# Weights queued behind x, activations behind state evictions, and an fp32 GLU with the normaliser's products among its blocks

## The chip, the cores and the metric

The kernel runs on one core of a Trainium2 chip. A core has a matrix engine (TensorE, PE in the rows, with its weight loads as PEld), three vector-like engines (VectorE = DVE, ScalarE = ACT, GpSimd = POOL), and SyncE (SP), which here only issues DMAs. Each engine works its own queue in order; semaphores tie the queues together, and 16 DMA engines carry the transfers. The metric is the device time of one execution, in microseconds (us): 1270.35 before the change, the median of 3 runs (1269.5 to 1273.52).

## The reference

One encoder layer on 256 positions with 16 learned meta tokens ahead (L = 272), model width 2048, all in float32:

```
hn = rmsnorm(h, norm_mix_g)
u_s5, qk_in, v_in, o_pre, gates_pre = split(hn @ w_in)      # 1024, 1024, 1024, 1024, 32 columns
# S5 half: 64 groups of 16 inputs, 64 complex states, a forward and a backward scan
y = s5_scan(u, fwd) + s5_scan(u, bwd) + d_skip * u
y = gelu(y)
y_s5 = rmsnorm(y * sigmoid(y @ w_glu + b_glu), s5_out_g)    # w_glu: 1024 x 1024
# mLSTM half: 8 heads, q and k of 64, v of 128, both directions
qk = silu(dwconv3(qk_in))
h_ml = (num_fwd / max(|den|, exp(-m))) + the same backward, then per-head rms norm, * head_g
y_ml = sigmoid(o_pre) * h_ml
h = h + concat(y_s5, y_ml) @ w_out                          # 2048 x 2048
hn = rmsnorm(h, norm_ffn_g)
h = h + (silu(dwconv3(hn @ w_gate)) * (hn @ w_up)) @ w_down # width 5632
return rmsnorm(h, final_g)[16:]
```

## The kernel before

Activations are kept transposed: 128 features on the partitions, positions along the free axis. A weight matrix comes in pieces of 128 x 1024 floats (512 KB), eight 128 x 128 blocks each. Products with weights are done in one of two ways. `whole` (L311 to L326) loads a piece and uses it as plain fp32; the trace shows each such product as two records. `stream` and `piece` (L232 to L250) load a piece as `raw`, ScalarE copies it into `hi` in the rounded type f32r (L247), VectorE forms `lo = raw - hi` (L248), and `mm3` does three f32r products, hi\*hi, hi\*lo, lo\*hi (L263 to L265). Both take their buffers from the same nine slots (three tags of three).

The order of work is not written out by hand. The framework's scheduler gives each engine a queue: it follows the order of the program as a priority, `hp()` raises the priority of what stands in it, and `behind(a, b)` puts a after b in an order without making it wait for b's result. A queue is then worked strictly in order.

The stages that the change touches, in order of time:

- *The start.* x comes as X in four quarters (`x_load`, L301), the first in two parts; `pd` is the last of these loads. ScalarE squares each (L308), VectorE scales it by g_mix (L310), the tables of the S5 recurrence are worked out from `par`, R (the norm's factor) is formed, and X is multiplied by it (L1002). `whole` loads the pieces of w_in for the first blocks; only its third piece is put behind `pd`.
- *Blocks of w_in* (`win_block`, L475: 16 fp32 products of 128 x 128 by 128 x 272, 32 records). Eight `u_block`s feed the S5 half: their result goes through `un` (L520 to L527) to DRAM (`ud`) and back as U, one pair of blocks at a time. `qk_block` (L658 on) gives a block of q or k: ScalarE evicts it twice (L665, L666), VectorE does the convolution `qt` (L668, L669), ScalarE takes SiLU into `q_sb` (L671) or `kE`, `kO`.
- *Input products of the S5* (`s5_in`, that is `in_coefs` and `in_proj`). `in_coefs` loads `tcf` (L534, a ring of two buffers, two loads each) and VectorE forms the coefficients `ic` (L542, `pp` L543). `in_proj` does 64 small products with U (L562) and ScalarE evicts them into the state ST (L568). They run in pairs m = 0,1 to 6,7.
- *The recurrence* on VectorE: `rec_local` (steps L575 to L578), `rec_carry` (L598 to L601), `rec_spread`.
- *Gate rows.* `gate_rows` (L615 on) forms the mLSTM's gate rows and sends them through DRAM: `nmd` (L638), `nmm` (L640, two), `cmd` (L649, two) and back as cM (L650, two; VectorE adds a constant to it, L651). `ml_meta` (L709 on) reads `nb` and `nb2` from `nmm` (L722, L723) and takes two exps, `pm` (L726, L727). Although this stands late in the program, the scheduler does it as soon as its data is there, around 55 to 77 us.
- *The heads* (`ml_head`), and then the GLU of the S5 half. `s5_gelu` takes the GELU of U in place and keeps it also as an f32r pair `yg`. `s5_glu` does eight blocks of eight `mm3` steps, a sigmoid, a product with U (L962), a split into y5 (L286) and a running sum of squares.
- *The normaliser* `ml_norm`, a generator (L787 on). Its first step sends the reciprocals to DRAM (`rd`). Each of the next eight loads `rb`, multiplies a head's `num` by it on VectorE (L800), adds the two directions on GpSimd, squares on ScalarE (L803) and sums with a product on TensorE (L804). All eight are called behind `s5_glu`.
- *w_out, first half*: 16 blocks of eight `mm3` steps with y5. The other half and the FFN follow.

## Time and profile before

| | before |
|---|---|
| median of 3 runs | 1270.35 us |
| the profiled execution: its time | 1271.38 us |
| its span, first to last instruction | 1269.6 us |
| mean granted TensorE clock | 0.984 |
| busy: PE, PEld | 1212.6 us (96%), 1082.7 us (85%) |
| busy: DVE, ACT, POOL | 796.1 us (63%), 535.3 us (42%), 221.6 us (17%) |
| chain that ended last | PE 79%, DVE 13%, DMA 4%, issue 2%, ACT 2% |

Busy is the time in which an engine has at least one instruction in work, waiting not counted; matmuls are pipelined, so records overlap. An idle time in front of an instruction is put down to what released it ("<-ACT ST L568" is the eviction in line 568 on ScalarE). The granted clock is the share of full speed that TensorE was allowed in a stretch; full is 2.4 GHz and the lower level 1.2. Engine averages hide the stages, since the limit changes along the program: so the rows further down are read by stretch.

### The profile page before, as it was taken

To read this page: it belongs to the slowest core of one execution; us is meant where nothing else is said; L and a number is where in the kernel's file an instruction comes from. 1 tells how busy PE (TensorE), PEld (TensorE's weight loads), DVE (VectorE), ACT (ScalarE), POOL (GpSimd) and SP (SyncE) were. 2 spreads that over 40 slices of the span, in tenths; PEclk is the share of its full clock that TensorE was granted. 3 is DMA by queue.
4 is the path that set the end of the run, shared out by engine and by line. 5 is a ranking of instruction groups with operands and counts; after the bars stand their busy time and mean duration, and the time that the engine had idled before them with its cause. 6 is when DMAs were issued, how large, how long until landed. Compare 5 with 4: busy or idle time off the path is not lost.

```text
span 1269.6 us, 21964 instructions
## 1 busy us (share of the span) xinstructions
PE 1212.6 (96%) x8865; PEld 1082.7 (85%) x8865; DVE 796.1 (63%) x1094; ACT 535.3 (42%) x865; POOL 221.6 (17%) x325
## 2 busy tenths in 40 slices
PE   5889997999998999999999999999999999999995
PEld 3768786787787799999999998889999999998884
DVE  4845999441238778766666665555666666665554
ACT  2622221125444546544444444334444444445542
POOL 3400000011315433122111220000221122111111
PEclk9989999999998999999999999999999999999998
DMA  8496544464345565555555556666555555556663
GB/s 316 128 302 195 186 148 140 125 183 133 92 133 176 161 191 183 182 185 181 188 186 184 184 184 184 193 185 198 185 187 185 183 183 183 185 177 195 188 190 112
DMA packets 84410, 227.79 MB, mean 179 GB/s; under 512 B 16508, under 2 KB 31380, under 8 KB 84308
## 3 DMA queue, kind: packets, MB, share of 16 engines
q1 hardware_dynamic: 76404, 220.67, 54.8%
q0 software_dynamic: 896, 3.28, 0.8%
q10 hardware_dynamic: 7008, 2.43, 0.8%
q8 instruction: 70, 1.15, 0.4%
q14 instruction: 32, 0.26, 0.1%
HBM read 219.81 MB, written 5.48 MB: 177 GB/s over the span
## 4 chain that ended last, share of the span: by engine, by line
PE 79%; DVE 13%; DMA 4%; issue 2%; ACT 2%; SPq 0%; DVEq 0%; POOL 0%; ACTq 0%
PE ps_mm L274 26%; PE ps_mm L275 13%; PE ps_mm L264 8%; PE ps_mm L475 8%; PE ps_mm L263 8%; PE ps_mm L265 8%; DMA tcf<-td 1%; PE ps_s L264 1%; PE ps_s L263 1%; PE ps_s L265 1%; DVE ST L578 1%; DVE t L576 1%; PE ps_s L886 1%; DVE t L575 1%; DVE ST L577 1%
## 5 line engine op out<-in xcount | busy, mean ns | idle before, releaser
L248 DVE TENSOR_TENSOR lo<-raw,hi 128x1024 fp32r<-128x1024 f32 (+1 forms) x312 | 393.5, 1261 | 233.0 <-ACT hi L247 226.9
L247 ACT ACTIVATE hi<-raw 128x1024 fp32r<-128x1024 f32 (+1 forms) x312 | 324.0, 1038 | 398.3 <-PE ps_mm L274 174.7
L475 PE MATMUL ps_mm<-X,wf 128*128 128x272 f32 (+1 forms) x1056 | 260.3, 405 | 18.7 <-DVE X L310 9.8
L475 PEld LDWEIGHTS ps_mm<-X,wf 128*128 128x128 f32 x1056 | 204.9, 197 | 62.0 <-DVE X L310 19.1
L274 PE MATMUL ps_mm<-X,hi 128*128 128x512 f32 x704 | 251.7, 399 | 0.0
L274 PE MATMUL ps_mm<-a,hi 128*128 128x512 f32 x704 | 244.1, 390 | 0.0
L264 PE MATMUL ps_mm<-X,hi 128*128 128x258 f32 x704 | 200.5, 285 | 0.0
L263 PE MATMUL ps_mm<-X,hi 128*128 128x258 f32 x704 | 199.1, 283 | 0.0
L275 PE MATMUL ps_mm<-a,lo 128*128 128x256 f32 x704 | 198.6, 282 | 0.0
L275 PE MATMUL ps_mm<-X,lo 128*128 128x256 f32 x704 | 198.1, 281 | 0.0
L265 PE MATMUL ps_mm<-X,lo 128*128 128x258 f32 x704 | 197.8, 281 | 0.0
L274 PEld LDWEIGHTS ps_mm<-X,hi 128*128 128x128 f32 x704 | 132.2, 188 | 30.1
L274 PEld LDWEIGHTS ps_mm<-a,hi 128*128 128x128 f32 x704 | 132.2, 188 | 27.6
L1144 POOL TENSOR_TENSOR gt<-gt,R 128x256 f32<-128x256 f32 x44 | 59.6, 1355 | 488.8 <-ACT gt L1143 488.8
L265 PEld LDWEIGHTS ps_mm<-X,lo 128*128 128x128 f32 x704 | 134.8, 191 | 0.0
L275 PEld LDWEIGHTS ps_mm<-X,lo 128*128 128x128 f32 x704 | 134.2, 191 | 0.0
L263 PEld LDWEIGHTS ps_mm<-X,hi 128*128 128x128 f32 x704 | 132.5, 188 | 1.9
L275 PEld LDWEIGHTS ps_mm<-a,lo 128*128 128x128 f32 x704 | 133.4, 190 | 0.0
L264 PEld LDWEIGHTS ps_mm<-X,hi 128*128 128x128 f32 x704 | 132.9, 189 | 0.0
L1149 DVE TENSOR_TENSOR u<-ps_mm,gt 128x512 f32<-128x512 f32 x44 | 30.4, 692 | 29.2 <-PE ps_mm L275 27.4
L1150 POOL TENSOR_TENSOR gt<-u 128x256 f32<-128x256 f32 x44 | 34.8, 790 | 40.5 <-DVE u L1149 40.5
L1138 DVE TENSOR_TENSOR gx<-ps_mm,R 128x258 f32<-128x258 f32 x44 | 18.8, 427 | 27.3 <-PE ps_mm L265 27.3
(333 smaller groups left out, 1401.9 us busy)
## 6 DMA issues: line engine op xcount, KB each, us to landing
raw<-wg SPq DMA_DIRECT2D x88, 512.0 KB, 3.9
raw<-wu SPq DMA_DIRECT2D x88, 512.0 KB, 4.2
wf<-win SPq DMA_DIRECT2D x65, 512.0 KB, 4.0
raw<-wd SPq DMA_DIRECT2D x64, 512.0 KB, 3.6
raw<-wout SPq DMA_DIRECT2D x32, 512.0 KB, 4.1
raw<-wd SPq DMA_DIRECT2D x32, 384.0 KB, 3.8
tcf<-td SPq DMA_DIRECT2D x16, 256.0 KB, 6.9
bc<-bcs SPq DMA_DIRECT2D x8, 512.0 KB, 3.7
```

Source lines behind the costliest of these rows:

```text
L247: S.activation(hi[:, a:b], raw[:, a:b], AF.Copy)
L248: V.tensor_tensor(out=lo[:, a:b], in0=raw[:, a:b], in1=hi.bitcast(F32)[:, a:b], op=ALU.subtract)
L263: nc.tensor.matmul(out_ap, h, xh, start=(first and i == 0), stop=False)
L264: nc.tensor.matmul(out_ap, h, xl, start=False, stop=False)
L265: nc.tensor.matmul(out_ap, l, xh, start=False, stop=(last and i == n - 1))
L274: nc.tensor.matmul(both[:, :, :cols], h, x, start=(i == 0), stop=False)
L275: nc.tensor.matmul(both[:, 1, :cols], l, x[:, 0, :], start=False, stop=(i == n - 1))
L475: last_o[0] = nc.tensor.matmul(p[:, :L - t0], w[k // 8][:, k % 8 * P:k % 8 * P + P], X[:, k, t0:], start=(k == 0), stop=(k == KD - 1))
L1138: V.tensor_tensor(out=x[:, :N], in0=p[:, :N], in1=R2, op=ALU.mult)
L1144: G.tensor_tensor(out=t, in0=t, in1=R2[:, 2:], op=ALU.mult)
L1149: V.tensor_tensor(out=u, in0=p.rearrange("p (j t) -> p j t", j=2), in1=t.unsqueeze(1).to_broadcast([P, 2, SEQ]), op=ALU.mult)
L1150: G.tensor_tensor(out=t, in0=u[:, 0, :], in1=u[:, 1, :], op=ALU.add)
```

## The change

1. `whole` puts its third to tenth piece behind the last load of x, where before it was the third alone.
2. `in_coefs` keeps its last `tcf` load in `last_tc`, and `gate_rows` puts `nmd`, `nmm` and `cmd` behind it. The loads of cM, `nb` and `nb2` read what those write, so they go with them.
3. `in_proj` keeps its last eviction of ST in `last_st`. `qk_block` no longer takes its SiLU itself but returns a function `act` that does, behind `last_st`; it is called behind the input products of the pair. The exp of `pm` is put behind `last_st` too.
4. `s5_gelu` no longer makes the f32r pair. `s5_glu` takes w_glu through `whole` and does one fp32 product of 128 x 128 by 128 x 272 a step, straight from U, instead of three in f32r.
5. From its fourth block on, `s5_glu` calls the normaliser once a block (five times); three calls stay behind it.

Lines from there on are numbered 2 to 5 higher in the changed kernel.

```diff
@@ -230,2 +230,4 @@
     last_o = [None]
+    last_st = [None]
+    last_tc = [None]
 
@@ -323,3 +325,3 @@
             last_raw[0] = nc.sync.dma_start(w[:, a:b], src[:, a:b])
-            if plain[0] == 3:
+            if 3 <= plain[0] <= 10:
                 behind(last_raw[0], pd)
@@ -533,5 +535,5 @@
         for g in range(2):
-            nc.sync.dma_start(t[64 * g:64 * g + 64].rearrange("p q r k -> p (q r k)"),
-                              tb["td"][:, g, 4 * m:4 * m + 4].rearrange("s j d r p -> s (j d r p)")
-                              .unsqueeze(0).to_broadcast([16, 4, 1024]))
+            last_tc[0] = nc.sync.dma_start(t[64 * g:64 * g + 64].rearrange("p q r k -> p (q r k)"),
+                                           tb["td"][:, g, 4 * m:4 * m + 4].rearrange("s j d r p -> s (j d r p)")
+                                           .unsqueeze(0).to_broadcast([16, 4, 1024]))
         if m >= 4:
@@ -567,3 +569,3 @@
                 j = 4 * m + q0 + o
-                S.copy(ST[:, 2 * j:2 * j + 2, :, 1:], pv[o])
+                last_st[0] = S.copy(ST[:, 2 * j:2 * j + 2, :, 1:], pv[o])
 
@@ -637,5 +639,5 @@
         nmm = dr.tile([2, 8, 16, L], F32, name="nmm")
-        nc.sync.dma_start(nmd, M[:40])
+        behind(nc.sync.dma_start(nmd, M[:40]), last_tc[0])
         for d in range(2):
-            nc.sync.dma_start(nmm[d], M[32 * d:32 * d + 8].unsqueeze(1).to_broadcast([8, 16, L]))
+            behind(nc.sync.dma_start(nmm[d], M[32 * d:32 * d + 8].unsqueeze(1).to_broadcast([8, 16, L])), last_tc[0])
         cT = lq.tile([P, 2, 40], F32, name="cT")
@@ -648,3 +650,3 @@
         for d in range(2):
-            nc.sync.dma_start(cmd[d], c[32 * d:32 * d + 8, 0:16])
+            behind(nc.sync.dma_start(cmd[d], c[32 * d:32 * d + 8, 0:16]), last_tc[0])
             nc.sync.dma_start(cM[:, d:d + 1], cmd[d].rearrange("h (s o) -> (h s) o", o=1))
@@ -669,7 +671,10 @@
             V.scalar_tensor_tensor(out=tt, in0=x[:, t0 + 2:L + 2], scalar=vc("qw", 16 + m), in1=tt, op0=ALU.mult, op1=ALU.add)
-        if m < 4:
-            S.activation(q_sb[:, m, :], t[:, T0:], AF.Silu)
-        else:
-            S.activation(kE[0:64, m - 4, :], t[0:64], AF.Silu)
-            S.activation(kO[64:128, m - 4, :], t[64:128], AF.Silu)
+
+        def act():
+            if m < 4:
+                behind(S.activation(q_sb[:, m, :], t[:, T0:], AF.Silu), last_st[0])
+            else:
+                behind(S.activation(kE[0:64, m - 4, :], t[0:64], AF.Silu), last_st[0])
+                S.activation(kO[64:128, m - 4, :], t[64:128], AF.Silu)
+        return act
 
@@ -725,3 +730,3 @@
         cM = rows["cM"]
-        S.activation(pm[:, 1:N], nb[:, 1:N], AF.Exp, bias=cM[:, 0:1])
+        behind(S.activation(pm[:, 1:N], nb[:, 1:N], AF.Exp, bias=cM[:, 0:1]), last_st[0])
         S.activation(pm[:, N + 1:N + 2], nb2[:, 1:2], AF.Exp, bias=cM[:, 1:2])
@@ -938,13 +943,6 @@
     def s5_gelu(m):
-        if m == 0:
-            s5["yg"] = l2b.tile([P, 2, 8, L], F32R, name="yg")
-        yg = s5["yg"]
         g = ysl(m)
-        yv = lambda i: yg[:, i, m, :].rearrange("p (t c) -> p t c", t=T)
         S.activation(g, g, AF.Gelu_apprx_tanh)
-        S.copy(yv(0), g)
-        V.tensor_tensor(out=yv(1), in0=g, in1=yv(0).bitcast(F32), op=ALU.subtract)
 
     def s5_glu():
-        yg = s5["yg"]
         y5 = l2a.tile([P, 2, 8, L], F32R, name="y5")
@@ -952,7 +950,9 @@
         for b in range(4):
-            get = stream(A["wglu"][b], 16)
             for i in range(2):
                 m = 2 * b + i
+                with hp():
+                    w = whole(A["wglu"][b][:, 1024 * i:1024 * i + 1024])
                 p = bank(("mm", "s5")[m % 2])
-                mm3(p[:, :L], get, lambda k: (yg[:, 0, k, :], yg[:, 1, k, :]), 8, 8 * i)
+                for k in range(8):
+                    s5["last"] = nc.tensor.matmul(p[:, :L], w[:, k * P:k * P + P], ysl(k), start=(k == 0), stop=(k == 7))
                 sg = r1m("sg")
@@ -969,2 +969,4 @@
                     G.tensor_tensor(out=acc, in0=acc, in1=sq, op=ALU.add)
+                if m > 2:
+                    next(nrm)
         pa = bank("s5")
@@ -1003,8 +1005,8 @@
         if m % 2 and m > 1:
-            qk_block((m - 3) // 2)
+            act = qk_block((m - 3) // 2)
             s5_in(m - 3)
             s5_in(m - 2)
+            act()
     rec_local(tb, 0)
-    qk_block(3)
-    qk_block(4)
+    act3, act4 = qk_block(3), qk_block(4)
     s5_in(6)
@@ -1012,2 +1014,4 @@
     s5_in(7)
+    act3()
+    act4()
     rec_spread(tb, 0)
@@ -1028,3 +1032,3 @@
     for m in range(5, 8):
-        qk_block(m)
+        qk_block(m)()
     for h in range(5):
@@ -1071,3 +1075,3 @@
     s5_glu()
-    for h in range(8):
+    for h in range(3):
         next(nrm)
```

SyncE at the start of the program, before: the pieces of w_in (`wf`) and the parts of x (`X`).

```order
L323 DMA wf<-win 128x256
L323 DMA wf<-win 128x1024 x2
L323 DMA wf<-win 128x768
L301 DMA X<-xt 128x544
L301 DMA X<-xt 128x1088
L456 DMA par<-par 128x384
L323 DMA wf<-win 128x1024 x3
L301 DMA X<-xt 128x1088 x2
L323 DMA wf<-win 128x1024 x3
```

After:

```order
L325 DMA wf<-win 128x256
L325 DMA wf<-win 128x768
L303 DMA X<-xt 128x544
L303 DMA X<-xt 128x1088
L458 DMA par<-par 128x384
L325 DMA wf<-win 128x1024
L303 DMA X<-xt 128x1088 x2
L325 DMA wf<-win 128x1024 x7
```

Four pieces of 128 x 1024 that stood ahead of the last two loads of x now stand behind them.

ScalarE around the first pair of input products, before. `qx` and `qt` evict the first block of q, `ST` are the evictions of the input products, `pm` is the exp and `q_sb` the SiLU.

```order
L726 ACTIVATE pm<-nb,cM 128x257
L727 ACTIVATE pm<-nb_2626,cM 128x1
L665 COPY qx<-ps_mm 128x258
L666 ACTIVATE qt<-ps_mm,vec 128x258
L568 COPY ST<-ps_s_481 128x4x67
L568 COPY ST<-ps_s_482 128x4x67
L671 ACT_TABLE_LOAD
L671 ACTIVATE q_sb<-qt 128x258
L568 COPY ST<-ps_s_501 128x4x67
L568 COPY ST<-ps_s_502 128x4x67
L568 COPY ST<-ps_s_530 128x4x67
L568 COPY ST<-ps_s_531 128x4x67
```

After:

```order
L667 COPY qx<-ps_mm 128x258
L668 ACTIVATE qt<-ps_mm,vec 128x258
L570 COPY ST<-ps_s_480 128x4x67
L570 COPY ST<-ps_s_481 128x4x67
L570 COPY ST<-ps_s_500 128x4x67
L570 COPY ST<-ps_s_501 128x4x67
L570 COPY ST<-ps_s_529 128x4x67
L570 COPY ST<-ps_s_530 128x4x67
L570 COPY ST<-ps_s_549 128x4x67
L570 COPY ST<-ps_s_550 128x4x67
L675 ACT_TABLE_LOAD
L675 ACTIVATE q_sb<-qt 128x258
```

Both exps have left the stretch, and the SiLU with the load of its table stands behind the pair's eight evictions.

SyncE behind the sixth `u_block`, after the change: the gate rows' loads, which before stood among the `tcf` loads of the first pairs.

```order
L536 DMA tcf<-td 64x1x1024 x4
L640 DMA nmd<-gM 40x272
L325 DMA wf<-win 128x1024
L642 DMA nmm<-gM 128x1x272 x2
L651 DMA cmd<-gc 8x16 x2
L727 DMA nb<-nmm 128x258
L325 DMA wf<-win 128x1024
L652 DMA cM<-cmd 128x1 x2
L728 DMA nb_2609<-nmm 128x2
```

They follow the last four loads of `tcf` now, with pieces of w_in between them.

VectorE in the GLU, before. `lo` are the low parts of weights, `sgt` and `y_` belong to the GLU's blocks, `num` are the normaliser's products with rb.

```order
L248 TENSOR_TENSOR lo<-raw,hi 128x1024
L962 TENSOR_TENSOR sgt<-sg,U 128x272
L286 SCALAR_TENSOR_TENSOR y_3040<-sgt,vec,y_3040 128x272
L248 TENSOR_TENSOR lo<-raw,hi 128x1024
L962 TENSOR_TENSOR sgt<-sg,U 128x272
L800 TENSOR_TENSOR num<-num,rb 128x516
L248 TENSOR_TENSOR lo<-raw,hi 128x1024
L286 SCALAR_TENSOR_TENSOR y_3040<-sgt,vec,y_3040 128x272
L800 TENSOR_TENSOR num<-num,rb 128x516
L962 TENSOR_TENSOR sgt<-sg,U 128x272
L800 TENSOR_TENSOR num<-num,rb 128x516
L248 TENSOR_TENSOR lo<-raw,hi 128x1024
```

After:

```order
L962 TENSOR_TENSOR sgt<-sg,U 128x272
L288 SCALAR_TENSOR_TENSOR y_3023<-sgt,vec,y_3023 128x272
L805 TENSOR_TENSOR num<-num,rb 128x516
L962 TENSOR_TENSOR sgt<-sg,U 128x272
L805 TENSOR_TENSOR num<-num,rb 128x516
L250 TENSOR_TENSOR lo<-raw,hi 128x1024
L805 TENSOR_TENSOR num<-num,rb 128x516
L288 SCALAR_TENSOR_TENSOR y_3023<-sgt,vec,y_3023 128x272
L805 TENSOR_TENSOR num<-num,rb 128x516 x3
L962 TENSOR_TENSOR sgt<-sg,U 128x272
L805 TENSOR_TENSOR num<-num,rb 128x516 x2
```

Most of the subtractions for `lo` are gone from between them. TensorE in the same place, after the change; before, all eight products of the normaliser (L804) stood among those of w_out.

```order
L957 MATMUL ps_mm<-U,wf 128x272 x8
L957 MATMUL ps_s_3045<-U,wf 128x272 x8
L957 MATMUL ps_mm<-U,wf 128x272 x8
L957 MATMUL ps_s_3085<-U,wf 128x272 x8
L809 MATMUL ps_acc<-hsq,er 40x258
L957 MATMUL ps_mm<-U,wf 128x272 x8
L809 MATMUL ps_acc<-hsq,er 40x258
L957 MATMUL ps_s_3140<-U,wf 128x272 x8
L809 MATMUL ps_acc<-hsq,er 40x258
L957 MATMUL ps_mm<-U,wf 128x272 x8
L809 MATMUL ps_acc<-hsq,er 40x258
L957 MATMUL ps_s_3194<-U,wf 128x272 x8
L809 MATMUL ps_acc<-hsq,er 40x258
```

The normaliser's first five products stand among the blocks of the GLU, from behind its fourth block on.

## Rows read from the trace of the kernel before

**Rows 1.** Windows: stretch, length; each engine's busy us (records); PEclk, DMA share, GB/s.

```profile
10.00:20.00 10.00, 4.81 (x10) 3.21 (x11) 4.12 (x6) 2.57 (x3) 2.47 (x1) 1.00 1.02 410
75.00:85.00 10.00, 4.93 (x133) 3.74 (x130) 5.64 (x8) 5.15 (x14) 0.90 (x1) 0.80 1.03 328
111.00:219.00 108.00, 101.36 (x678) 83.24 (x676) 105.14 (x204) 21.60 (x61) 2.37 (x13) 0.99 0.49 159
368.67:380.88 12.21, 12.21 (x98) 12.21 (x97) 6.31 (x7) 7.65 (x14) 0.00 (x0) 1.00 0.87 277
380.88:399.47 18.59, 14.42 (x99) 13.76 (x97) 16.89 (x18) 7.23 (x13) 12.65 (x11) 0.91 0.72 216
399.47:460.73 61.26, 56.80 (x405) 51.49 (x403) 47.16 (x58) 29.46 (x47) 25.99 (x27) 0.94 0.52 163
449.26:455.00 5.74, 5.74 (x51) 5.74 (x50) 3.79 (x5) 2.12 (x2) 2.14 (x3) 1.00 0.76 236
```

**Rows 2.** Timeline, SyncE, start: start, length, engine, line, operation, count [idle before, releaser].

```profile
5.81 2.26 SPq L323 DMA_DIRECT2D wf<-win  x3
10.17 1.57 SPq L301 DMA_DIRECT2D X<-xt  x2
```

**Rows 3.** Timelines of VectorE, ScalarE and TensorE, from x to the first blocks.

```profile
20.34 7.60 DVE L310 TENSOR_SCALAR X<-X,vec 128x272 f32<-128x272 f32 x8 [2.21 <-ACT sqx L308]
...
38.59 1.28 ACT L290 ACT_TABLE_LOAD   x1
...
42.38 7.67 DVE L1002 TENSOR_TENSOR X<-X,R 128x272 f32<-128x272 f32 x15
...
43.49 30.89 PE L475 MATMUL ps_mm<-X,wf 128*128 128x272 f32 x128 [3.41 <-ACT tkc L398]
```

**Rows 4.** Timeline of TensorE, first and second pair of input products.

```profile
74.85 1.16 PE L562 MATMUL ps_s<-U,ic 64*64 64x67 f32 x64 [0.47 <-DMA U<-ud]
...
83.34 1.44 PE L562 MATMUL ps_s<-U,ic 64*64 64x67 f32 x32 [3.80 <-ACT ST L568]
84.72 22.53 PE L475 MATMUL ps_mm<-X,wf 128*128 128x272 f32 x92
107.18 1.16 PE L562 MATMUL ps_s<-U,ic 64*64 64x67 f32 x64
...
110.98 20.98 PE L475 MATMUL ps_mm<-X,wf 128*128 128x272 f32 x92
```

**Rows 5.** Timelines of ScalarE and VectorE around the first pair.

```profile
76.20 0.51 ACT L726 ACTIVATE pm<-nb,cM 128x257 f32<-128x257 f32 x1 [7.66 <-DMA nb<-nmm]
...
82.60 0.42 ACT L671 ACTIVATE q_sb<-qt 128x258 f32<-128x258 f32 x1 [3.13 <-DVE qt L669]
...
80.42 1.23 DVE L543 TENSOR_TENSOR pp<-tcf,ST 128x1024 f32<-128x1024 f32 x1 [4.25 <-issue]
```

**Rows 6.** Timelines of VectorE and TensorE in the GLU and w_out's first half.

```profile
382.58 0.70 DVE L800 TENSOR_TENSOR num<-num,rb 128x516 f32<-128x516 f32 x1 [4.44 <-DMA rb<-rd]
...
395.07 0.59 PE L265 MATMUL ps_s<-yg,lo 128*128 128x272 f32 x1 [2.52 <-DVE lo L248]
...
415.00 0.63 PE L804 MATMUL ps_acc<-hsq,er 128*40 128x258 f32 x2
...
442.14 0.39 PE L265 MATMUL ps_mm<-y,lo 128*128 128x258 f32 x1 [2.47 <-DVE lo L248]
```

**Rows 7.** Timeline of VectorE in the recurrence, an add of the recurrence's second step.

```profile
121.48 1.29 DVE L577 TENSOR_TENSOR ST<-ST,t 128x1088 f32<-128x1088 f32 x1
```

**Rows 8.** Timeline of SyncE, the last four loads of tcf.

```profile
110.47 3.74 SPq L534 DMA_DIRECT2D tcf<-td  x4
```

**Rows 9.** cM's two loads before: how long they took to land.

```profile
DMA to landing us min/median/max: 7.5/7.9/8.3
```

**Rows 10.** tcf's loads from 100 to 140 us, how long they took to land.

```profile
DMA to landing us min/median/max: 3.1/3.4/3.7
```

**Rows 11.** TensorE from 111 to 131 us by line: busy us, mean ns of one.

```profile
L475 PE MATMUL ps_mm<-X,wf 128*128 128x272 f32 (+1 forms) x89 | 20.3, 390 | 0.0
```

## The prediction

> **What bounds the kernel now.** TensorE is busy in most of the span, but it is not the limit everywhere, and the change works where it is not. I read the chain of waits first (mostly TensorE, some VectorE), then the windows stage by stage [rows 1], and then the timelines of the stretches in which TensorE's sum fell short. Five places matter.
>
> *The start.* Nothing can run before x is there. From 10 to 20 us the core's 16 DMA engines are full (share 1.02, 410 GB/s) [rows 1], and SyncE has issues of w_in's pieces ahead of x's last two loads, three of them just before, and these go out at 10.17 us [rows 2]. VectorE's last scaling of X (8 instructions) starts at 20.34 after a wait for ScalarE's squares, and lasts 7.60; the S5 tables follow, ScalarE loads a table at 38.59, R comes, X\*R starts at 42.38 and the first long run of TensorE at 43.49 [rows 3].
>
> *The first pair of input products* (in_proj 0 and 1). It starts at 74.85 after 0.47 of waiting for U, and the next block of w_in starts at 84.72: 9.87 us. The second pair takes from 107.18 to 110.98, 3.80 us, for the same work [rows 4]. The difference lies in ScalarE's queue: the exp pm stood 7.66 us until nb had landed, then the SiLU q_sb stood 3.13 us for VectorE's qt, and VectorE itself came to the product pp only at 80.42 after 4.25 us idle [rows 5]. The evictions of the S5 state stand behind both; TensorE waited 3.80 for one of them at 83.34 [rows 4].
>
> *111 to 219 us:* VectorE is busy for 105.14 of 108.00 (the recurrence), so VectorE is the limit there [rows 1].
>
> *The GLU*, 368.67 to 399.47 us, 30.80 us in all: the first half of its blocks runs clean in 12.21, the second takes 18.59 with TensorE busy in 14.42 of it at a granted clock of 0.91 [rows 1]. VectorE's first product num\*rb waited 4.44 for rb until 382.58, and the lo parts of the weights stand behind those products: TensorE waited 2.52 for lo at 395.07 [rows 6].
>
> *The first half of w_out*, 399.47 to 460.73 us: 61.26 us, of which TensorE is busy 56.80, at a clock of 0.94. A clean pair of its 16 blocks takes 5.74 [rows 1], so 8 pairs need 45.9. The rest is the normaliser's products (two records of one in 0.63 at 415.00), waits for lo (2.47 at 442.14) [rows 6] and passes at the lower of the two clock levels (1.2 instead of 2.4 GHz), which follow such waits.
>
> Behind 460.73 TensorE runs at its own pace, and the change leaves the code of that part alone. So a gain before that point comes out at the end.
>
> **The change part by part.** The sum is made against the profiled execution: 1271.38 us, span 1269.6; the median of the runs is 1270.35, 1.0 below, and I don't correct for that.
>
> *Pieces behind x: -6.0.* The order of SyncE shows four more pieces of 512 KB moved behind x, 2.1 MB. At 410 GB/s [rows 1] that is 5.1 us of transfers that x no longer shares. SyncE's own time adds to it: three such issues took 2.26 us [rows 2], so x's last loads go out sooner too; I take 6.0. The steps between the last X and 43.49 [rows 3] are a chain in which each engine waits for the one before, so they move with x. The price is that weights land later; the first run of TensorE starts more than 20 us after they are issued, so they are hidden. Bounds: -3 (the tables have work of their own that doesn't wait for X) and -8 (7.6 of issue and transfer saved).
>
> *Evictions ahead of the activations, gate rows behind the tcf loads: -6.0.* With the SiLU and the two exps queued after the last eviction, ScalarE meets neither the wait of 7.66 nor that of 3.13 [rows 5] before it serves TensorE. The pair should take what the second pair took: 9.87 - 3.80 = 6.07 [rows 4]. What is late next is U (the wait of 0.47 is its tail [rows 4]) and tcf, for which VectorE's pp waits. U follows un and so moves with the start; tcf gains, because nmd, nmm, cmd, cM, nb and nb2 leave SyncE's queue ahead of it. Bounds: -3 and -6.
>
> *Clock: -1.5.* After the stall the granted clock is 0.80 in 75 to 85 us [rows 1], and the next 92 passes took 22.53 where the same 92 passes later took 20.98 [rows 4]: 1.55. With no stall the engine has no pause to fall in. Bounds 0 and -3 (the other end has the pair itself at the full clock).
>
> *A new wait: +3.0.* cM now comes behind all tcf loads, and VectorE's one addition to it stands within the recurrence, right behind the add that starts at 121.48 and lasts 1.29, to 122.77 [rows 7]. VectorE is the limit there [rows 1], so each us of waiting is lost, with the rest of the recurrence queued behind it and TensorE's S5 products waiting for that. In times of before: the last four tcf loads occupy SyncE from 110.47 to 114.2 [rows 8]. Behind them stand nmd, a weight piece, two nmm and two cmd; five issues at about 0.6 each (from the tcf rows: 3.74 holds a wait, so this is rough) put nmm's first at about 116. Then nb must wait until nmm has landed, and cM stands behind nb: two landings in a row. The nearest rows lie far apart: cM itself took 7.5 to 8.3 [rows 9] while the DMA engines were full, whereas in 100 to 140 us, where this chain now falls, tcf lands in 3.1 to 3.7 [rows 10]. I take the second, since it is that stretch: 116 + 3.5 + issues of 2.5 + 3.5 = 125.5, 2.7 behind 122.77; with a little for scattered 4-byte elements 3.0. Bounds 0 and +11 (two landings of 8: 116 + 8 + 2 + 8 = 134). ScalarE's second exp waits for nb2 in the same way, but what stands behind it there (un of the block u7) isn't due for several us: 0.
>
> *GLU in fp32: +2.4.* One block is now 8 products of two passes each. The nearest row is the same form in w_in, 89 passes in 20.3, 0.228 each [rows 11]; 16 of them make 3.65 a block, 14.6 for four, against 12.21 with f32r [rows 1]. No row has this form with U's strided view as the moving operand; 22.53/92 = 0.245 [rows 4] is the upper bound, +2.2 over 128 passes. The hi and lo copies fall away, so VectorE's lo wait inside the GLU is gone. But the normaliser's first five products now stand among TensorE's blocks. The first needs rb, which VectorE had at 382.58 with 0.70 for the product [rows 6], then GpSimd's add and a square: about 384.3. TensorE reaches it after four blocks at 368.67 + 14.6 = 383.3, waits 1.0, then runs four blocks (14.6) and five products of up to 0.6 (3.0; the pair of records at 415.00 took 0.63 [rows 6]): 401.9 against 399.47. Bounds +1 (no wait) and +6 (each product waits about 1 for its rb, and the wait makes the clock fall).
>
> TensorE showed 0.127 for an f32r product (12.21 over the 96 of four blocks) and 0.456 for a whole fp32 product, so 1.2 times three f32r products [rows 1, 11]. The Trainium skill, "FP8 and Floating Point Precision", section "TensorE Precision Notes", gives "True FP32: 4 passes through PE array", against three here; an estimate by that page would make the GLU's 24.4 into 32.5 instead of 29.2 and the end 3.3 later. The measured passes decide, and the later time is inside the range.
>
> *First half of w_out: -9.3.* Five of the eight products have left; VectorE reaches w_out's lo parts sooner since its products num\*rb are done in the GLU, where no lo needs it. 8 pairs 45.9, three products 1.8, and I keep the wait of 2.47 at 442.14 [rows 6] with about 1.7 of slow clock behind it, 4.2: 51.9 against 61.26. Bounds -4 (lo bunched up behind other products as before) and -12 (no wait left at all, less the products).
>
> *Heads:* eight copies and eight subtractions of the GELU output go, from engines that are not the limit there: 0.
>
> Sum: -6.0 - 6.0 - 1.5 + 3.0 + 2.4 - 9.3 = -17.4; 1271.4 - 17.4 = **1254.0**.
>
> **The rivals.** *B, the gain at the input products is taken by another wait ahead of them.* For it: the DMA engines are full in 75 to 85 us (share 1.03) [rows 1], so taking small loads out of tcf's way may not bring tcf forward, and x may land no sooner if its loads share the engines with the weights anyway. Against it: the stall names nb and qt, not U or tcf. The pair then keeps about 6 of its 7.5 (with the clock): 1254.0 + 6 = 1260.
>
> *C, cM lands late in the recurrence.* For it: its own rows say 7.5 to 8.3 [rows 9], and both landings are in series. Against it: what tcf does in that stretch [rows 10]. VectorE waits 11 instead of 3: 1262.
>
> *E, the GLU part brings nothing.* The wait for rb is paid by TensorE in the order of its queue instead of by VectorE, and lo bunches up again at w_out's head, so that w_out gains about 3 instead of 9.3: 1254.0 + 6.3 = 1260.3. For it: rb is late in any case [rows 6]. Against it: VectorE is busy 16.89 of 18.59 there [rows 1], and the subtractions for the GLU's lo leave it.
>
> *D, slower than before.* The chain of C grows further: it decides from 17.4 + 3.0 = 20.4 us of VectorE's waiting, that is, if the chain nmm, nb, cM ended after about 122.77 + 20.4 = 143 [rows 7]. From 116 that would be two landings of 12, half as long again as the slowest row [rows 9]; at 14 each the time is 1275.
>
> **How the numbers follow.** The forecast has 0.53, B 0.12, C 0.14, E 0.12, two of B, C and E together 0.05 (about 1268), D 0.04. The likeliest gives 1254.0. Its favourable ends that are likely together (start -8, no wait for cM, w_out -11.5) give about 1246.5; the single rivals lie at 1260 to 1262, and with their terms' unfavourable ends at up to 1265. The range is 1246 to 1265: it leaves out most of the joint case, D and the far ends. A measurement of this kernel can tell about 0.3%, 3.8 us, from no change. Faster by more than that takes in the forecast, B, C, E and a part of the joint case: 0.92; within it 0.04; slower 0.04.
>
> **What would show it.** In the changed kernel: X\*R begins at about 36.4 instead of 42.38; the first pair takes about 4 us from its first product to the next w_in block, with no ScalarE wait ahead of an eviction; the granted clock in it is near 1; VectorE's cM addition starts after some 3 us of idle time; the GLU takes some 33 us with one short wait of TensorE at its fifth block; the first half of w_out about 52. Wrong would be: X\*R where it was (x shares the engines), the pair at 8 us with U or tcf named (B), several waits of TensorE for hsq in the GLU and the lo waits of w_out still there (E), or an idle gap of VectorE ahead of the cM addition of some 11 us (C) or over 20 (D).

## The result, and the profile after

The changed kernel takes 1251.8 us, the median of 4 runs (1250.08 to 1254.58), against 1270.19 for the kernel before in the same measurement: a ratio of 0.9852 with a 95% interval of 0.9827 to 0.9877; the medians lie 18.4 us apart. Forecast were 1254.0, with a range of 1246 to 1265. The profiled execution took 1250.08, the quickest of its four, and that of before (1271.38) lies 1.2 above its median; so the two traces differ by 21.3 in their spans, and some 3 of that is which execution was profiled.

The page of the profile after (span, busy time of the engines, the chain that ended last):

```profile
span 1248.3 us, 21801 instructions
PE 1206.8 (97%) x8801; PEld 1075.5 (86%) x8801; DVE 782.1 (63%) x1078; ACT 530.8 (43%) x853; POOL 224.4 (18%) x325
PE 86%; DVE 10%; DMA 2%; issue 1%; SPq 1%; ACT 0%; DVEq 0%
```

TensorE does about the same work (1212.6 before), but the chain now runs over it for 86% of the span instead of 79%: more waits went than work. Where they went can be read off TensorE's timeline, since each stage begins with a record of its own. The timeline of TensorE, after, up to the second pair of input products (columns as in [rows 2]); these answer to [rows 3, 4]:

```profile
36.58 30.89 PE L477 MATMUL ps_mm<-X,wf 128*128 128x272 f32 x128 [5.05 <-ACT un L529]
67.39 1.16 PE L564 MATMUL ps_s<-U,ic 64*64 64x67 f32 x64
...
71.14 20.98 PE L477 MATMUL ps_mm<-X,wf 128*128 128x272 f32 x92
92.05 1.16 PE L564 MATMUL ps_s<-U,ic 64*64 64x67 f32 x64
...
95.80 20.98 PE L477 MATMUL ps_mm<-X,wf 128*128 128x272 f32 x92
```

The first pair takes 3.75 us (67.39 to 71.14) like the second, and the 92 passes behind it 20.98 instead of 22.53. The same engine later, after; the first two lines are the S5 output products, then come the GLU with the first of its normaliser's products, the last of the five, the start of w_out, and the one wait left in w_out's first half; the last line is the first record of the second half:

```profile
209.21 1.41 PE L891 MATMUL ps_s<-ST,c 64*64 64x68 f32 x38 [4.79 <-DVE c L866]
...
280.63 0.92 PE L891 MATMUL ps_s<-ST,c 64*64 64x68 f32 x42 [0.96 <-issue]
...
353.74 3.93 PE L957 MATMUL ps_mm<-U,wf 128*128 128x272 f32 x16
357.51 3.83 PE L957 MATMUL ps_s<-U,wf 128*128 128x272 f32 x16
...
368.60 0.63 PE L809 MATMUL ps_acc<-hsq,er 128*40 128x258 f32 x2
369.16 3.93 PE L957 MATMUL ps_mm<-U,wf 128*128 128x272 f32 x16
...
386.30 0.63 PE L809 MATMUL ps_acc<-hsq,er 128*40 128x258 f32 x2
386.86 0.39 PE L265 MATMUL ps_mm<-y,hi 128*128 128x258 f32 x1
...
417.87 0.39 PE L267 MATMUL ps_s<-y,lo 128*128 128x258 f32 x1 [2.15 <-DVE lo L250]
...
439.40 0.28 PE L265 MATMUL ps_mm<-yml,hi 128*128 128x258 f32 x1
```

Three records of before that the rows ahead of the prediction don't have (same columns): its S5 output products, and a wait in the heads.

```profile
219.90 1.40 PE L886 MATMUL ps_s<-ST,c 64*64 64x68 f32 x38 [6.49 <-DVE c L861]
292.79 0.87 PE L886 MATMUL ps_s<-ST,c 64*64 64x68 f32 x42 [1.00 <-issue]
317.75 0.60 PE L734 MATMUL ps_acc<-pm,cst 128*40 128x258 f32 x2 [2.14 <-ACT w L760]
```

With these the span falls apart into stages, each from the first record of one to the first of the next:

| stage on TensorE | before | after | difference | forecast |
|---|---|---|---|---|
| up to the first long run | 43.49 | 36.58 | -6.9 | -6.0 |
| long run, to the first pair | 31.36 | 30.81 | -0.55 | |
| first pair of input products | 9.87 | 3.75 | -6.1 | -6.0 |
| to the second pair | 22.46 | 20.91 | -1.55 | -1.5 |
| to the S5 output products (the recurrence) | 112.72 | 117.16 | +4.4 | +3.0 |
| S5 output products, first three groups | 72.89 | 71.42 | -1.5 | 0 |
| last group and heads | 75.88 | 73.11 | -2.8 | 0 |
| GLU | 30.80 | 33.12 | +2.3 | +2.4 |
| first half of w_out | 61.26 | 52.54 | -8.7 | -9.3 |
| the rest | 808.87 | 808.90 | 0 | 0 |
| sum | 1269.6 | 1248.3 | -21.3 | -17.4 |

The new wait is there too. VectorE's timeline in the recurrence, after, with SyncE's issues for it:

```profile
106.36 1.28 DVE L579 TENSOR_TENSOR ST<-ST,t 128x1088 f32<-128x1088 f32 x1
111.57 0.16 DVE L653 TENSOR_TENSOR cM<-cM,cst 128x1 f32<-128x1 f32 x1 [3.93 <-DMA cM<-cmd]
```

```profile
95.34 3.74 SPq L536 DMA_DIRECT2D tcf<-td  x4
...
100.22 1.54 SPq L642 DMA_DIRECT2D nmm<-gM  x2
101.87 4.81 SPq L651 DMA_DIRECT2D cmd<-gc  x2
106.78 0.35 SPq L727 DMA_DIRECT2D nb<-nmm  x1
...
108.00 0.79 SPq L652 DMA_DIRECT2D cM<-cmd  x2
```

VectorE stood 3.93 us for cM in the stretch in which it is the limit, and the stretch is 4.4 longer.

### The profile page after: what moved, and what is told of

Read it like the earlier page. It is cut to its first block, busy times and chain, and to the rows that moved or that the text cites. A ratio compares the mean times of both kernels' runs of the same rounds, so it can differ in the third digit from the quotient of the medians.

```text
span 1248.3 us, 21801 instructions
## 1 busy us (share of the span) xinstructions
PE 1206.8 (97%) x8801; PEld 1075.5 (86%) x8801; DVE 782.1 (63%) x1078; ACT 530.8 (43%) x853; POOL 224.4 (18%) x325
## 4 chain that ended last, share of the span: by engine, by line
PE 86%; DVE 10%; DMA 2%; issue 1%; SPq 1%; ACT 0%; DVEq 0%
PE ps_mm L276 26%; PE ps_mm L277 14%; PE ps_mm L477 11%; PE ps_mm L266 8%; PE ps_mm L265 8%; PE ps_mm L267 8%; PE ps_s L267 1%; PE ps_mm L957 1%; PE ps_s L957 1%; PE ps_s L265 1%; PE ps_s L266 1%; PE ps_s L891 1%; DVE ST L580 1%; DVE t L578 1%; DVE X L312 1%
## 5 line engine op out<-in xcount | busy, mean ns | idle before, releaser
L250 DVE TENSOR_TENSOR lo<-raw,hi 128x1024 fp32r<-128x1024 f32 (+1 forms) x304 | 380.9, 1253 | 227.1 <-ACT hi L249 226.9
L249 ACT ACTIVATE hi<-raw 128x1024 fp32r<-128x1024 f32 (+1 forms) x304 | 315.6, 1038 | 394.1 <-PE ps_mm L276 144.0
L477 PE MATMUL ps_mm<-X,wf 128*128 128x272 f32 (+1 forms) x1056 | 256.7, 401 | 20.1 <-DMA wf<-win 5.3
L769 DVE SCALAR_TENSOR_TENSOR w<-ps_s,w 128x256 f32<-128x256 f32 (+3 forms) x32 | 10.2, 355 | 57.2 <-ACT w L762 29.6
```

The costliest lines, as they stand in the source:

```text
L249: S.activation(hi[:, a:b], raw[:, a:b], AF.Copy)
L250: V.tensor_tensor(out=lo[:, a:b], in0=raw[:, a:b], in1=hi.bitcast(F32)[:, a:b], op=ALU.subtract)
L477: last_o[0] = nc.tensor.matmul(p[:, :L - t0], w[k // 8][:, k % 8 * P:k % 8 * P + P], X[:, k, t0:], start=(k == 0), stop=(k == KD - 1))
```

## The experiments

Each is the changed kernel with one thing altered (the last builds on the fourth). The kernel before ran beside them on the same chip and took 1270.83 beside the first four and 1272.21 beside the last four, where it had 1270.19 beside the changed kernel; so a difference to the changed kernel is taken from the two ratios to the kernel before, times 1270 (the first experiment: 0.9907 - 0.9852 = 0.0055, 7.0 us). The ratios' intervals are some 0.2% to either side, and a difference of two ratios carries both, some 4 us. So by the ratios alone the first, the third and the last experiment differ clearly from the changed kernel, the one with the addition on GpSimd barely, and the f32r GLU, the products behind the GLU and the kept copies not; what is said of those rests on the lengths of stages, each from one trace. The times that the last four expected were set against 1251.8, and there the kernel before took 0.16% longer, 2 us. In the profiles of the seven that keep the changed start, TensorE's first long run begins at 37.1 to 37.8, where the changed kernel's has 36.58: about 1 us of the start varies from run to run, so stages are compared by their lengths.

### The pieces ahead of x again

```diff
-            if 3 <= plain[0] <= 10:
+            if plain[0] == 3:
```

> The changed kernel with w_in's pieces ordered as before (only the third piece behind x). Theory: x lands later by the 2.1 MB ahead of it, so X*R starts near 42.4 instead of 36 us, everything behind is as in the changed kernel but later: +6 to +7 us, about 1258.5. Rival (the gain at the start came from another order of the tables on VectorE and ScalarE, not from x's transfers): X*R stays near 36 and the time within 2 us of 1251.8.

Measured: 1259.04, ratio 0.9907 (0.9887 to 0.9928): +7.0. TensorE's timeline of this kernel:

```profile
42.84 30.89 PE L477 MATMUL ps_mm<-X,wf 128*128 128x272 f32 x128 [3.22 <-ACT tkc L400]
75.63 1.16 PE L564 MATMUL ps_s<-U,ic 64*64 64x67 f32 x64 [1.90 <-DMA U<-ud]
```

The long run is back at 42.84, X\*R begins at 41.73 (35.95 in the changed kernel), and the first pair waits 1.90 for U on top of it. The theory holds: the start's gain is x's earlier landing. A late start thus also brings a wait for U, so the 0.55 of the second row of the table belongs to this part too; what held U up was not tried.

### The gate rows ahead of the tcf loads again

```diff
-        behind(nc.sync.dma_start(nmd, M[:40]), last_tc[0])
+        nc.sync.dma_start(nmd, M[:40])
...
```

(nmm and cmd likewise.)

> The changed kernel without the rule that puts nmd, nmm and cmd behind the last tcf load; the SiLU and the first exp stay behind the evictions. The second exp (pm from nb2) then stands ahead of the first pair's evictions on ScalarE, and the cM addition on VectorE ahead of that pair's last coefficient. Theory: cM's wait of 3.9 us in the recurrence goes, but the pair stalls again by some 5 us for nb2, with a slow clock behind it (1.5): net +2 to +4, about 1254.5. Rival (the SiLU's place alone removed the stall, the gate rows' place did nothing for it): the pair stays near 3.8 us and the 3.9 of the recurrence is gained: about 1248.

Measured: 1253.34, ratio 0.9857 (0.9843 to 0.9872): +0.6, no difference by the interval. Timelines of TensorE and of ScalarE, and a window over the pair (stretch, length, busy PE, PEld, DVE, ACT, POOL, granted clock, DMA share, GB/s):

```profile
70.41 1.40 PE L564 MATMUL ps_s<-U,ic 64*64 64x67 f32 x64 [2.24 <-DMA U<-ud]
...
74.06 0.49 PE L564 MATMUL ps_s<-U,ic 64*64 64x67 f32 x4 [1.05 <-ACT ST L570]
...
77.67 21.14 PE L477 MATMUL ps_mm<-X,wf 128*128 128x272 f32 x92
```

```profile
72.71 0.30 ACT L732 ACTIVATE pm<-nb,cM 128x1 f32<-128x1 f32 x1 [10.37 <-DMA nb<-nmm]
```

```profile
70.41:77.67 7.26, 6.21 (x133) 4.34 (x133) 2.82 (x3) 2.90 (x10) 0.90 (x1) 0.55 1.03 333
```

The pair takes 7.26 us (70.41 to 77.67), U is 2.24 late, and ScalarE stands 10.37 for nb ahead of the evictions. In the recurrence VectorE no longer waits for cM, and the way from the second pair to the output products is 112.77 instead of 117.16: 4.4 gained there, 5.6 lost (2.1 up to the pair, 3.5 in it). The rival falls: the SiLU's place alone doesn't remove the stall. The move of the gate rows bought 5.6 and paid 4.4 for it.

ScalarE's 10.37 is not what TensorE paid, though. TensorE waited 1.05 for an eviction; most of the other 2.5 is the granted clock, 0.55 over the pair (1.2 GHz would be 0.50) and low from its first record on (1.40 where the changed kernel has 1.16), that is, behind the wait for U. In the first experiment a wait of 1.90 for U was followed by a pair of 3.75 at a granted clock of 1.00; why the clock fell here and not there stays open.

### The SiLU in place again

```diff
-                behind(S.activation(q_sb[:, m, :], t[:, T0:], AF.Silu), last_st[0])
+                S.activation(q_sb[:, m, :], t[:, T0:], AF.Silu)
```

(at once in `qk_block`, for kE, kO and the first exp likewise.)

> The changed kernel with the SiLU taken inside qk_block again and the first exp free, the gate rows still behind tcf. Theory: the SiLU waits for VectorE's qt (which stands behind products on tcf) ahead of the evictions, so the first pair takes some 7 to 8 us instead of 3.75, with 1 to 1.5 of slow clock behind it: about 1256. Rival (only the exp's wait for nb stalled the pair, and it is away): the pair stays near 4 us, 1252.

Measured: 1259.99, ratio 0.991 (0.9891 to 0.9928): +7.4. Timelines of ScalarE and of TensorE:

```profile
75.17 0.42 ACT L675 ACTIVATE q_sb<-qt 128x258 f32<-128x258 f32 x1 [4.27 <-DVE qt L671]
```

```profile
75.92 1.44 PE L564 MATMUL ps_s<-U,ic 64*64 64x67 f32 x32 [4.47 <-ACT ST L570]
77.29 23.22 PE L477 MATMUL ps_mm<-X,wf 128*128 128x272 f32 x92
```

With no exp in the way at all, the pair takes 9.2 us (68.09 to 77.29), almost the 9.87 of before, and the passes behind it 23.22 instead of 20.98. So the wait for qt gives nearly the whole stall by itself (TensorE waits 4.47 for an eviction behind it), and the 7.66 that ScalarE stood for nb in the kernel before added some 0.7 to the pair. The gate rows' early place by itself costs 5.6 too, by U, an eviction and the clock, as the experiment before this one shows. The two don't add up, and a kernel that mends one alone keeps most of the stall. The theory expected 7 to 8 here and 1256; it was right in kind and some 3 us too low.

### The addition to cM on GpSimd

```diff
-        V.tensor_tensor(out=cM[:, 1:2], in0=cM[:, 1:2], in1=kc("mcol"), op=ALU.add)
+        G.tensor_tensor(out=cM[:, 1:2], in0=cM[:, 1:2], in1=kc("mcol"), op=ALU.add)
```

> The changed kernel with the addition to cM on GpSimd instead of VectorE, nothing else. Theory: VectorE is the limit in the recurrence, so the 3.9 us that it idles for cM come out at the end: S5's output products start some 3.9 earlier, about 1248. Rival (TensorE or ScalarE would be late there anyway, ScalarE's second exp waits 8.7 for the same loads): less than 1 us, 1251 to 1252.

Measured: 1248.48, ratio 0.9818 (0.9801 to 0.9834): -4.3. TensorE's timeline:

```profile
206.86 1.40 PE L891 MATMUL ps_s<-ST,c 64*64 64x68 f32 x38 [7.36 <-DVE c L866]
```

From the second pair (94.40) to here it is 112.46 instead of 117.16, so the 3.93 and a little more come out. VectorE is the limit of the recurrence, as the forecast had it, and the wait was a matter of which engine's queue it stood in.

### The GLU in f32r, the products still among its blocks

```diff
-                    w = whole(A["wglu"][b][:, 1024 * i:1024 * i + 1024])
...
-                    s5["last"] = nc.tensor.matmul(p[:, :L], w[:, k * P:k * P + P], ysl(k), start=(k == 0), stop=(k == 7))
+            get = stream(A["wglu"][b], 16)
...
+                s5["last"] = mm3(p[:, :L], get, lambda k: (yg[:, 0, k, :], yg[:, 1, k, :]), 8, 8 * i)
```

(and the f32r pair yg in `s5_gelu`.)

> The changed kernel with the GLU's three f32r products, its pair yg and its split pieces back, the normaliser's five products still among the blocks. Theory: what the change gains in w_out comes from two things, VectorE's lo work for w_glu gone and the products gone from w_out; with lo back, the GLU shows waits for lo or for hsq again (31 to 36 us against 33.1), w_out's first half loses a part of its 8.7 (54 to 58 us against 52.5), and the heads' stretch loses some 2.5 to the copies: 1254 to 1259. Rival (the products' place is the whole gain, fp32 is only dearer): GLU near 29, w_out near 52, 1248 to 1250.

Measured: 1257.61, ratio 0.9881 (0.9857 to 0.9905): +3.7. TensorE's timeline:

```profile
309.00 0.60 PE L740 MATMUL ps_acc<-pm,cst 128*40 128x258 f32 x2 [1.78 <-ACT w L766]
...
376.30 0.63 PE L810 MATMUL ps_acc<-hsq,er 128*40 128x258 f32 x2 [1.36 <-ACT hsq L809]
```

The time is where the theory put it, and so are w_out's half and the heads, but not the GLU, for which it had 31 to 36. It takes 29.4 us (359.92 to 389.31), less than in fp32, although five products stand in it and one of them waits 1.36; the first half of w_out takes 56.7. Together they make 86.1, against 85.7 in the changed kernel. What is lost lies ahead of them: the wait for w in the heads is back, and the stretch from 284.35 to 359.92 is 75.6 instead of 73.1.

### The products behind the GLU, fp32 kept

```diff
-                if m > 2:
-                    next(nrm)
...
-    for h in range(3):
+    for h in range(8):
```

> The changed kernel with the GLU in fp32 but all eight of the normaliser's steps behind it, so that its products stand in w_out again. Theory: the GLU gets shorter by the five products of 0.56 (about 30.3 us against 33.1) and w_out's first half longer by them; their place on TensorE is worth little by itself, but the chain that hangs behind the eighth product (rs, rsb, yml) starts later and its VectorE work falls on other lo parts: 1251 to 1254. Rival (the place is what freed w_out's lo): w_out back at 59 to 61 us, 1256 to 1258.

Measured: 1257.81, ratio 0.9884 (0.9857 to 0.9911): +4.1. The time lies nearer the rival's, but with its interval it doesn't decide; the stages do, and the theory falls. The GLU is 29.2 (355.75 to 384.98), w_out's first half 61.3, as long as before. But the rival's reason (lo) is not what the trace shows: TensorE's waits for lo in this half are 2.2 in all, and 2.15 in the changed kernel. TensorE and VectorE of this kernel, and a window (stretch, length, PE, PEld, DVE, ACT, POOL busy, granted clock, DMA share, GB/s):

```profile
388.93 0.39 PE L265 MATMUL ps_mm<-y,hi 128*128 128x258 f32 x1 [1.19 <-ACT y L287]
```

```profile
367.62 0.70 DVE L805 TENSOR_TENSOR num<-num,rb 128x516 f32<-128x516 f32 x1 [5.63 <-DMA rb<-rd]
...
391.69 1.01 DVE L288 SCALAR_TENSOR_TENSOR y<-sgt,vec,y 128x272 fp32r<-128x272 f32 x1
```

```profile
390.00:396.00 6.00, 5.25 (x22) 4.76 (x23) 2.71 (x3) 2.64 (x4) 0.87 (x2) 0.58 0.26 90
```

And VectorE of the changed kernel, the same two instructions:

```profile
365.64 0.70 DVE L805 TENSOR_TENSOR num<-num,rb 128x516 f32<-128x516 f32 x1 [5.65 <-DMA rb<-rd]
...
389.77 1.02 DVE L288 SCALAR_TENSOR_TENSOR y<-sgt,vec,y 128x272 fp32r<-128x272 f32 x1
```

In both kernels VectorE waits 5.6 for rb, then works through eight products with rb and the rest of the GLU's splits, and the last split of y5 ends 25.1 us after rb's landing (367.62 to 392.70, and 365.64 to 390.79). That tail doesn't depend on where TensorE has the products: VectorE is busy for most of it, with some 2.5 to 3 us of short waits between, nearly all for ScalarE, which works on the same blocks in turn with it. TensorE without the five products gets to w_out some 4 us sooner, finds y not there, waits 1.19 and several times less (2.4 in all for y and hi), and is then granted 0.58 of its clock from 390 to 396, in the first passes of w_out. With the products among the blocks it does them in that time, and w_out begins with no wait. So the products' place is worth 4.9 us (85.7 against 90.5 for both stages); as these traces read, it gains not by freeing lo but by filling a time in which TensorE would have stood anyway and then run at a low clock.

### The copies kept, unread

```diff
         S.activation(g, g, AF.Gelu_apprx_tanh)
+        S.copy(yv(0), g)
+        V.tensor_tensor(out=yv(1), in0=g, in1=yv(0).bitcast(F32), op=ALU.subtract)
```

> The changed kernel, but s5_gelu still makes the f32r pair, which nothing reads: eight copies on ScalarE and eight subtractions on VectorE come back. Theory: the stretch between the S5 output products and the GLU gained 2.8 us that the forecast put at nothing, of which 2.1 is a wait of TensorE for ScalarE's w early in the heads; with the copies back that wait is back: 1253.5 to 1255. Rival (the wait went with the three w_glu pieces that the heads no longer split): 1251 to 1252.

Measured: 1256.16, ratio 0.9875 (0.9851 to 0.9899): +2.9. TensorE's timeline:

```profile
308.06 0.60 PE L739 MATMUL ps_acc<-pm,cst 128*40 128x258 f32 x2 [2.07 <-ACT w L765]
```

The wait early in the heads is back, 2.07, and the stretch of the last group and the heads is 75.9 (283.12 to 358.98) instead of 73.1. The rival (the w_glu pieces) falls, by the stage: the ratios' +2.9 fits its 2.8, but is not clear of noise by itself.

### The last steps of the normaliser spread over w_out

On top of the addition on GpSimd:

```diff
-            V.tensor_tensor(out=rb, in0=num[h][:, 0, :], in1=rb, op=ALU.mult)
+            behind(V.tensor_tensor(out=rb, in0=num[h][:, 0, :], in1=rb, op=ALU.mult), last_lo[0])
...
     for h in range(3):
         next(nrm)
-    for _ in nrm:
-        pass
...
+        for h in range((0, 0, 0, 1, 2, 2, 2, 1)[m]):
+            next(nrm)
```

(`last_lo` is the last subtraction for lo; the last two lines stand at the end of each pair of w_out's blocks.)

> The kernel with the cM addition on GpSimd (1248.5) and one more change: the normaliser's last steps (product with rsb, GpSimd, split of yml) are called one or two for each pair of w_out's blocks from the fourth pair on, each behind that pair's lo, where VectorE did all eight in one bunch with w_out's lo parts stuck between them. Theory: TensorE's wait of 2.2 to 2.5 us for lo in the middle of w_out's first half and the slow clock behind it go, the half takes about 49 us: 1244 to 1245.5. Rival (VectorE has no room there in any order, or the last yml comes late for the second half): the wait moves, 1248 or later.

Measured: 1243.67 (1242.53 to 1245.27), ratio 0.9777 (0.9756 to 0.9798): -9.5, and 5.2 below the kernel with the addition on GpSimd alone. The windows in the middle of w_out's first half, in the changed kernel and then here:

```profile
416.00:422.00 6.00, 4.13 (x23) 4.13 (x24) 6.00 (x9) 2.98 (x5) 4.21 (x5) 0.75 0.39 137
```

```profile
415.00:421.00 6.00, 6.00 (x53) 6.00 (x51) 5.70 (x9) 3.08 (x5) 3.26 (x2) 1.00 0.67 209
```

VectorE has about as much to do in both, but here lo comes first, TensorE stays busy at the full clock, and the half takes 49.3 (385.31 to 434.62) instead of 52.5; the kernel that this one builds on had 53.3. What is left of the waits is 0.58 for lo near the end. It is the quickest version here.

## Why the prediction was right, point by point

**Pieces behind x (-6.0): right, -6.9 in the table.** The first experiment gives 7.0 by its ratio. Some of the closeness is chance: against the 43.49 of before, the seven other kernels with this start gain 5.7 to 6.4. The forecast left out the wait for U (0.47 before, 1.90 in the first experiment) that goes as well.

**Evictions ahead (-6.0) and the clock (-1.5): right, -6.1 and -1.55.** The pair of [rows 4] was a good measure of itself: what the second pair took, the first took. The forecast treated SiLU and gate rows as one term, and the experiments show that it had to: with either one put back alone the pair takes 3.5 or 5.5 longer, with both (the kernel before) 6.1. As a reading of the stall it was loose: ScalarE's two waits, 7.66 and 3.13, are not shares of it, since without the first the pair still takes 9.2. What the sum would have got wrong is a kernel with only one of the two.

**The new wait (+3.0): right in place and cause, somewhat too small.** VectorE stood 3.93 and the stretch grew by 4.4. The choice between the landing of [rows 9] and that of [rows 10] decided this term; the stretch's own row was the right one. From the end of the tcf issues (99.08) to cM it took 12.5 us, where the forecast's chain had 11.3. SyncE issued nb 7.7 behind the tcf issues, where the chain had 5.3; ahead of it stand the two cmd issues, which took 4.81 where the forecast had about 0.6 an issue. nmm's landing is not in the trace, so which of the two held nb is not shown.

**GLU (+2.4): right in the sum, +2.3, wrong in the parts.** Four blocks take 14.86 (forecast 14.6), so U's strided view costs nothing against [rows 11]: a block every 3.67, 0.229 a pass. No product waits for hsq (forecast 1.0), since hsq is there before the fourth block ends. But a product of the normaliser costs more than its 0.56: the block behind it takes 3.86 instead of 3.67, and the five make the GLU 3.9 longer than in the kernel that has none there (33.12 against 29.2), where the forecast had 3.0. An fp32 product of the GLU (0.458) takes 1.2 times three f32r products (0.381), as the rows of before said. The Trainium skill ("FP8 and Floating Point Precision", "TensorE Precision Notes") counts four passes for true FP32; the estimate from that, against three f32r products, is 1.33. The trace does not agree, and the time went by the measured passes.

**First half of w_out (-9.3): right in size, -8.7, with the wrong reason behind it.** Beside the five products, the forecast gave the gain to VectorE: less lo in the way. GLU and w_out's first half together took 92.1 before, 90.5 with fp32 alone, 86.1 with the products' place alone and 85.7 with both; so of the 6.4 the place gives 4.9 to 6.0 and fp32 0.4 to 1.5. The step that failed is "VectorE reaches w_out's lo parts sooner" as the reason. VectorE did end its GLU work sooner (the last split of y5 ends 40.3 us behind the GLU's first product before, 37.1 after), but with fp32 alone it does so too (37.0), and w_out's half stays at 61.3; and TensorE's waits for lo there went only from 2.9 to 2.15. VectorE's end is set by rb's landing in every version (25.1 to 26.4 behind it), and what changed is that TensorE does the products meanwhile and so neither stands for y nor starts w_out at a slow clock. The wait for lo that the forecast kept (2.47) is there, 2.15 at 417.87.

**Heads (0): wrong, -2.8.** "From engines that are not the limit there" was read from an average. ScalarE is busy for half of that stretch, yet its copies stood ahead of and among the heads' first w, for one of which TensorE waited 2.14 at 317.75 in the trace of before. Where that happens ScalarE is nearly full, 15.15 of 17.00 us (a window of before):

```profile
301.00:318.00 17.00, 14.86 (x98) 12.73 (x93) 5.13 (x15) 15.15 (x34) 3.34 (x6) 1.00 0.40 112
```

That row was there to be read. The experiments also show that with the products among the GLU's blocks this is nearly all that fp32 is worth: without it (f32r, 86.1) and with it (85.7) the two stages take about the same, but f32r needs the copies.

**S5 output products (0): -1.5, and not by the change.** The stretch doesn't follow the wait for c ahead of it: the kernel with the gate rows early waits 7.37 and takes 71.90, the one with the SiLU in place waits 4.23 and takes 72.45. It follows the clock granted in the ten us behind that wait, 0.60 before and 0.75 in the changed kernel, the lowest and the highest of the ten traces, with 0.62 to 0.68 and 71.9 to 72.9 in the experiments (windows of before and of the changed kernel, columns as above):

```profile
219.90:229.90 10.00, 10.00 (x144) 7.56 (x145) 5.20 (x7) 0.95 (x3) 0.00 (x0) 0.60 0.28 99
```

```profile
209.21:219.21 10.00, 10.00 (x150) 7.89 (x151) 6.62 (x11) 0.95 (x3) 0.00 (x0) 0.75 0.29 104
```

What sets how long the clock stays low there was not tried. The experiments' kernels have the same code there, so most of the 1.5 is luck of the two traces.

**The rivals.** B (another wait at the pair) did not come, C (cM late by 11) did not come either (3.93), nor did E (no gain in the GLU part; it gave 6.4) or D. The forecast for the time was 2.2 us too high. 1.2 of that is where it started, from the profiled 1271.4 and not from the median 1270.2; by the medians the gain is 18.4 against 17.4. That is closer than the terms are: in the two traces the heads, the S5 output products and the start gave 5.7 more than forecast, and the wait for cM and w_out 2.0 less.

## What to carry to other kernels

Two waits ahead of the same work on one in-order queue are not worth the sum of their lengths, nor each its own: price them together, by a stretch that has neither, and don't expect a wait's length from mending it alone. An instruction that waits for a late transfer belongs in the queue of an engine that has time at that point: a 0.16 us addition held the limiting engine for 3.9. Small work of the engine that will soon have to wait is best placed ahead of that wait, and steps of a later stage behind, not among, the work that the present stage's limit depends on.

## What the runs showed of the hardware

VectorE's product num\*rb takes 0.68 to 0.70 when no addition of GpSimd is in work as it starts, and 1.07 to 1.26 when one is, in the kernel before and the changed one; y's split takes 0.50 and 0.88 to 1.04 in the same way. What counts in these rows is the start: the product at 376.52 begins 0.07 ahead of a GpSimd addition, runs beside it and takes 0.70, and the split behind it, which starts while that addition is in work (376.59 to 377.84), takes 1.00. What is added is somewhat less than the addition still has to run: 0.50 of 0.71 there, 0.37 of 0.53 at 366.91. The times of GpSimd are rough in the profile. That makes VectorE's tail behind rb longer than the sum of its undisturbed parts, and it was not tried by itself. VectorE and GpSimd of the changed kernel:

```profile
366.91 1.07 DVE L805 TENSOR_TENSOR num<-num,rb 128x516 f32<-128x516 f32 x1
...
376.52 0.70 DVE L805 TENSOR_TENSOR num<-num,rb 128x516 f32<-128x516 f32 x1 [0.61 <-DMA rb<-rd]
377.13 1.00 DVE L288 SCALAR_TENSOR_TENSOR y<-sgt,vec,y 128x272 fp32r<-128x272 f32 x1
...
379.73 0.50 DVE L288 SCALAR_TENSOR_TENSOR y<-sgt,vec,y 128x272 fp32r<-128x272 f32 x1 [0.59 <-ACT y L287]
```

```profile
366.42 1.02 POOL L806 TENSOR_TENSOR num<-num 128x258 f32<-128x258 f32 x1 [17.98 <-DVE num L805]
...
376.59 1.25 POOL L969 TENSOR_TENSOR s5acc<-s5acc,sq 128x272 f32<-128x272 f32 x1
```

And a wait of TensorE that is short by itself is dear where the clock falls behind it: in the kernel with the products behind the GLU some 2 us of waiting at the head of w_out were followed by six at 0.58 of the full clock. It doesn't always fall: behind the wait of 1.90 for U in the kernel with the pieces ahead of x, the pair ran at a granted clock of 1.00.
